# Time mixing on one core: low ranks from u and its shift difference, without their mixtures

## The chip, the cores and the metric

One core of a Trainium2 chip runs the whole program as one launch. The metric is device time in microseconds (us). The kernel before takes 2986.44 us, the median of 3 runs (2984.91 to 2988.6).

## What is computed

Two blocks follow each other on 512 tokens of width 1024, all in fp32. The change lies in the second block's first layer, in its time mixing; this is the part of it that matters:

```python
def rwkv7_time_mix(x, mu, w_rkv, w_o, w0, w1, w2, a0, a1, a2, g1, g2, ...):
    x_prev = jnp.pad(x, ((0, 0), (1, 0), (0, 0)))[:, :-1]
    xx = x_prev - x
    xr, xw, xk, xv, xa, xg = [x + xx * mu[i] for i in range(6)]
    r, k, v = xr @ w_rkv[0], xk @ w_rkv[1], xv @ w_rkv[2]
    w = -jax.nn.softplus(-(w0 + jnp.tanh(xw @ w1) @ w2)) - 0.5
    a = jax.nn.sigmoid(a0 + (xa @ a1) @ a2)
    g = jax.nn.sigmoid(xg @ g1) @ g2
    ...
```

`x` is the normalised input (`u` in the kernel) and `xx` its difference to the token before (`d`). w1 and a1 are 1024 x 64, g1 is 1024 x 128: these are the low ranks. After that a recurrence runs over the tokens for 16 heads of 64 (a matrix of state per head), its output is normalised per head, multiplied by `g`, and goes through the output projection `w_o`.

## The kernel before

**Layout and precision.** Activations lie as 8 chunks of 128 channels by 512 tokens. A large matmul is made of three passes in fp32r: a weight tile `wr` of 128 x 1024 comes by DMA, ACT rounds it to `wh`, DVE or POOL subtracts to get the rest `wl` (`wload`, line 406), and an activation is split into two halves in the same way. The low ranks go as plain fp32 matmuls, which the trace shows as two records each. All DMAs stand in one queue, SP's.

**An order that a planner writes.** The tasks are Python generators (`_Emit`, line 88 on). The main stream (the projections) emits its matmuls, and before each it lets other tasks that are due by the planner's own estimates emit theirs. So the order of the instructions on every engine, and in SP's queue, is fixed when the program is built; an instruction that is not ready holds up everything behind it on its engine. PSUM tiles of the main stream are called `m`, those of the tasks `t`. Tiles of 128 x 512 fp32, called `a`, come from a pool of 56 (`NA`, line 26); tasks that need many wait for room in it.

**Time mixing** (`rwkv`, from line 1096) goes over two halves of 256 tokens. `norm_task` (1137) makes for each half and chunk a tile with `u` in its first 256 columns and `d` in the others (`ud`). `ORDER` (1108) is the order of the projections: K, W, A, R, V, G of half 0, then of half 1. `mix_task` (1160) makes the mixtures u + mu*d, at most 8 tiles ahead of their use, on DVE by `mix_chunk` (1121): into `h` with a split for K, R and V, into half of an `a` tile without one for W, A and G. `token_major` (1185) projects K and V, `receptance` (1666) R, `lora1` (1203) the low ranks W, A and G from the mixtures, 8 matmuls each and half, 64 wide for W and A and 128 for G:

```python
for k in range(DC):
    x_ = take(hf, i, k)[0]
    w_ = w[k * m // 512][:, k * m % 512 : k * m % 512 + m]
    em.need(ps[:m, HW], w_, x_)
    mm(ps[:m, HW], w_, x_, k == 0, k == DC - 1)
```

The main loop (line 1724) walks through `ORDER`, loads low-rank weights one step ahead, and spawns `keys_task`, `decay_task`, `a_task`, `g_task` and `values_task`, which finish the projections and write them to DRAM.

**The recurrence** is a chain of tasks. `prep` (1358), for each of four blocks of 128 tokens `j` and each half of the heads `q`, fetches keys, `a`, decay and R (its first fetch is `a<-kkt`), makes products on DVE and PE, and writes `fsc`; it starts when the pool has room for 12 tiles (line 1524) and the one before the last is done. `inverse` (1451) reads `fsc` for both `q` as `iat`, runs 62 small operations on POOL, each after the one before, writes the result as `xsc`, reads it back, and finishes on PE with 32 x 32 matmuls. `scan_task` (1577) passes the state from chunk to chunk on tiles `sv`, `gn_task` (1531) normalises. Blocks 0 and 1 are half 0. `w_o` (1698) of half 0 needs both blocks of half 0 through `gn_task`; its matmuls carry `rwkv_w_o` in `wh`. `post` (1687) adds and normalises, and the feed-forward part of the layer follows, whose stages keep PE nearly full.

Below, stages are named by projection and half: K0, W0, A0, R0, V0, G0 and K1 to G1.

Of the kernel before, what the change touches and what calls it, by code (L numbers as in the profile page):

```python
# [20 lines left out]
P = 128  # L21
T = 512
D = 1024
DC = D // P
# [10 lines left out]
_VEC = {}  # L35
# [52 lines left out]
class _Emit:  # L88
# [209 lines left out]
def tile_net(ctx: ExitStack, tc: tile.TileContext, a: dict, out: bass.AP, dbg=None, stop=None):  # L298
# [101 lines left out]
    def copy(out_, in_, scale=None):  # L400
        if scale is None:
            act.activation(out=out_, in_=in_, func=AF.Copy)
        else:
            act.activation(out=out_, in_=in_, func=AF.Copy, scale=scale)
# [157 lines left out]
    t_ = H()  # L562
    gp.memset(t_, 0.0)
    copy(t_[:, 0:1], t_[:, 0:1])
    ps = PS()
# [531 lines left out]
    def rwkv(on_h):  # L1097
# [2 lines left out]
        live[0] = BEFORE  # L1100

        ud = {}
        oka, half_tile = S(), [None]
        vt.tensor_scalar(out=oka[:, 0:8], in0=vec[:, _VEC["k_a"] : _VEC["k_a"] + 8], scalar1=-1.0, scalar2=1.0, op0=MUL, op1=ADD)
        R_, W_, K_, V_, A_, G_ = range(6)
        LORA = {W_: ("w1", 64), A_: ("a1", 64), G_: ("g1", 128)}

        ORDER = [(0, K_), (0, W_), (0, A_), (0, R_), (0, V_), (0, G_), (1, K_), (1, W_), (1, A_), (1, R_), (1, V_), (1, G_)]
        LAST_A = [x for x in ORDER if x[0] == 0][-1]
        mixed = {x: [] for x in ORDER}  # L1110
        made, used, flags = [0], [0], {}
        AHEAD = 8
        EARLY = 10
        MARGIN = [2]
        turn = [0]

# [4 lines left out]
        def mix_chunk(i, c, hf):  # L1121

            uc, dc, m = ud[hf, c][:, 0:256], ud[hf, c][:, 256:512], V("mu", 8 * i + c)
            if i in LORA:
                if c % 2 == 0:
                    half_tile[0] = A()
                t_ = half_tile[0][:, HALF[c % 2]]
                vt.scalar_tensor_tensor(out=t_, in0=dc, scalar=m, in1=uc, op0=MUL, op1=ADD)
                return (t_,)
            t_ = H()  # L1130
            vt.scalar_tensor_tensor(out=t_, in0=dc, scalar=m, in1=uc, op0=MUL, op1=ADD)
            x_ = A(F32R)
            hi, lo = x_[:, 0:256], x_[:, 256:512]
            split_into((hi, lo), t_, HW, eng=vt if c % 3 == 2 else gp)
            return hi, lo
# [22 lines left out]
                free(*h, n=2)  # L1158

        def mix_task():  # L1160
            for hf, i in ORDER:
                for c in range(DC):
                    while made[0] >= used[0] + (AHEAD if (hf, i) in ORDER[:4] else 8) or (hf, c) not in ud or not room(MARGIN[0]):
                        yield 0.25
                    mixed[hf, i].append(mix_chunk(i, c, hf))
                    made[0] += i not in LORA or c % 2
                    if hf == 1 and i == ORDER[-1][1]:
                        free(ud[1, c])
                    if hf == 0 and (hf, i) == LAST_A:
                        free(ud[0, c])  # L1170
                    yield mixed[hf, i][max(c - 2, 0)]

        for hf in range(2):
# [7 lines left out]
        def take(hf, i, k):  # L1181
            em.until(lambda: len(mixed[hf, i]) > k)
            return mixed[hf, i][k]
# [16 lines left out]
            mixed[hf, i] = None  # L1200
            return pss

        def lora1(w, m, hf, i):
            ps = PS()
            for k in range(DC):
                x_ = take(hf, i, k)[0]
                w_ = w[k * m // 512][:, k * m % 512 : k * m % 512 + m]
                em.need(ps[:m, HW], w_, x_)
                mm(ps[:m, HW], w_, x_, k == 0, k == DC - 1)
                if k % 2:  # L1210
                    used[0] += 1
                    free(x_)
            mixed[hf, i] = None
            return ps

        def kkrow(wh):
# [58 lines left out]
            free(x_)  # L1275
            flags["lg", hf] = True

        def load_raw(src, n, rows=P):

            ts = [A() for _ in range(0, n, 512)]  # L1280
            for i, t_ in enumerate(ts):
                dma(out=t_[:rows, :], in_=src[:, 512 * i : 512 * i + 512])
            return ts

        def lora2(hf, w, rows, mid, done_):
            ws = load_raw(a[w], 1024, rows)
            for n in range(DC):
                p2 = PS()
                w_ = ws[n // 4][0:rows, (n % 4) * 128 : (n % 4 + 1) * 128]
                yield (p2, w_, mid)  # L1290
                mm(p2[:, HW], w_, mid[0:rows, :])
                done_(n, p2)
            free(*ws)

        def a_task(hf, ps):

            x_ = A()
            mid = x_[:, HW]
            copy(mid[0:64, :], ps[0:64, HW])

            def fin(n, p2):
                t_ = H()
                act.activation(out=t_, in_=p2[:, HW], func=AF.Sigmoid, bias=V("a0", n))
                spill(ad[hf][n], t_)

            yield from lora2(hf, "a2", 64, mid, fin)
            free(x_)
            flags["a", hf] = True

        def g_task(hf, ps):  # L1310

            x_ = A()
            mid = x_[:, HW]
            act.activation(out=mid, in_=ps[:, HW], func=AF.Sigmoid)

            def fin(n, p2):
                t_ = H()
                copy(t_, p2[:, HW])
                spill(gd[hf][n], t_)

            yield from lora2(hf, "g2", 128, mid, fin)
            free(x_)
            flags["g", hf] = True

# [394 lines left out]
            free(*(zq[hf, k][i] for k in range(4) for i in range(2)))  # L1719
            em.spawn(post(hf, o, hs, so))  # L1720

        tasks = {W_: decay_task, A_: a_task, G_: g_task}
        raw = {}
        for n, (hf, i) in enumerate(ORDER):
            for nxt in ORDER[n : n + 2]:
                if nxt[1] in LORA and nxt not in raw:
                    w, m = LORA[nxt[1]]
                    raw[nxt] = load_raw(a[w], 8 * m)
            if not hv and n >= EARLY and min(done["z"]) >= 1:
                w_o(0)  # L1730
            if i in LORA:
                em.spawn(tasks[i](hf, lora1(raw[hf, i], LORA[i][1], hf, i)))
                free(*raw[hf, i])
            elif i == K_:
                em.spawn(keys_task(hf, token_major(a["w_k"], K_, hf)))
            elif i == V_:
                em.spawn(values_task(hf, token_major(a["w_v"], V_, hf)))
            else:
                receptance(hf)
                if hf == 0:  # L1740
                    for q in range(2):
                        em.spawn(scan_task(q))
# [313 lines left out]
def _wn(w, ncol=512):  # L2056

    k, n = w.shape
    return np.ascontiguousarray(w.reshape(k // 128, 128, n // ncol, ncol).transpose(2, 1, 0, 3).reshape(n // ncol, 128, -1))
# [6 lines left out]
def pack(inp):  # L2066
    g = {k: np.asarray(v) for k, v in inp.items()}
    w = {}
# [44 lines left out]
    w["w_k"] = _wn(rkv[1])  # L2113
    w["w_v"] = _wn(rkv[2])
    w["rwkv_w_o"] = _wt(g["rwkv_w_o_2"][0])
    w["w1"] = _wn(g["rwkv_w1_2"][0], 64)[0]
    w["w2"] = np.ascontiguousarray(np.concatenate([g["rwkv_w2_2"][0], g["rwkv_w0_2"][0][None]], axis=0))
    w["a1"] = _wn(g["rwkv_a1_2"][0], 64)[0]
    w["a2"] = np.ascontiguousarray(g["rwkv_a2_2"][0])
    w["g1"] = _wn(g["rwkv_g1_2"][0], 128)[0]  # L2120
    w["g2"] = np.ascontiguousarray(g["rwkv_g2_2"][0])
# [28 lines left out]
```

## Time and profile before

| | |
|---|---|
| median of 3 runs | 2986.44 us |
| the profiled execution's own time | 2986.91 us |
| its span | 2985.1 us |
| PE busy | 2820.6 us (94%) |
| DVE, ACT, POOL busy | 1624.0, 1233.9, 692.3 us |
| mean granted TensorE clock | 0.968 of 2.4 GHz |

The profile is of one execution. Busy time is the time in which an engine had an instruction running; matmuls are pipelined and their ends are modelled, so a busy PE is not PE at its peak. The granted clock is 1 where TensorE ran at 2.4 GHz and 0.5 where it ran at 1.2 GHz; a value between is a mixture over the stretch. A wait is put down to the engine whose work was the last to be ready.

### The profile page before, as it was taken

What the parts mean: (1) busy time and instruction counts of PE and PEld (TensorE: products, weight loads), DVE (VectorE), ACT (ScalarE), POOL (GpSimd) and SP (SyncE); (2) the same over time, 40 slices, a digit from 0 to 9 for tenths busy, and PEclk for the clock granted to TensorE, in tenths of its full rate; (3) what the DMA queues carried; (4) which work ended last, traced back from release to release, by engine and by line L of the source; (5) the groups of instructions that cost most, each with busy time, mean ns of one, the idle gap of its engine ahead of it and who ended that gap; (6) DMA issues with size and microseconds to landing.
All of it is one profiled execution on the core that took longest, in us unless ns stands there. A gap on an engine that the chain in (4) does not pass through costs nothing. (4 is left out here: it accounts for less than half of the span.)

```text
span 2985.1 us, 45687 instructions
## 1 busy us (share of the span) xinstructions
PE 2820.6 (94%) x17736; PEld 2442.6 (82%) x17736; DVE 1624.0 (54%) x2896; ACT 1233.9 (41%) x2141; POOL 692.3 (23%) x802
## 2 busy tenths in 40 slices
PE   9999999999999989878789989998999989999998
PEld 7788888889888877656679989998888877888887
DVE  6545443335334486955676665366234476852336
ACT  4532333333333345544455544344233347733333
POOL 0022211111111143444355110111111134420111
PEclk9999999999999999988889999999999999999999
DMA  5333333332333455645565556343334432323334
GB/s 187 88 94 97 114 99 99 98 95 81 108 99 121 121 184 185 205 142 159 166 177 167 179 168 180 111 145 111 98 98 122 124 114 75 102 80 101 111 109 155
DMA packets 179408, 378.31 MB, mean 127 GB/s; under 512 B 57204, under 2 KB 81908, under 8 KB 179192
## 3 DMA queue, kind: packets, MB, share of 16 engines
q1 hardware_dynamic: 179192, 375.40, 41.6%
q8 instruction: 140, 2.29, 0.3%
q14 instruction: 76, 0.62, 0.1%
HBM read 342.04 MB, written 29.36 MB: 124 GB/s over the span
## 5 line engine op out<-in xcount | busy, mean ns | idle before, releaser
L379 PE MATMUL m<-a,wh 128*128 128x256 f32 (+1 forms) x8512 | 2061.5, 334 | 15.1 <-DVE a L290 7.2
L379 PEld LDWEIGHTS m<-a,wh 128*128 128x128 f32 x8512 | 1461.6, 192 | 178.7 <-issue 13.9
L379 PE MATMUL m<-a,wl 128*128 128x256 f32 (+1 forms) x4256 | 1414.1, 333 | 2.9 <-DVE wl L290 2.9
L290 ACT ACTIVATE wh<-wr 128x1024 fp32r<-128x1024 f32 (+2 forms) x585 | 606.0, 1038 | 1190.7 <-PE m L379 714.8
L290 DVE TENSOR_TENSOR wl<-wr,wh 128x1024 fp32r<-128x1024 f32 (+2 forms) x547 | 679.7, 1244 | 458.9 <-ACT wh L290 456.0
L379 PEld LDWEIGHTS m<-a,wl 128*128 128x128 f32 x4256 | 815.8, 192 | 78.4 <-DVE wl L290 3.5
L290 POOL TENSOR_TENSOR a<-a,a 128x256 f32<-128x256 f32 (+5 forms) x312 | 359.6, 1159 | 1633.5 <-ACT a L290 1317.4
L290 DVE TENSOR_TENSOR a<-m,a 128x512 f32<-128x512 f32 (+1 forms) x324 | 198.5, 614 | 629.6 <-PE m L379 618.9
L290 ACT ACTIVATE a<-a 128x512 f32<-128x512 f32 (+6 forms) x515 | 239.6, 481 | 121.3 <-DVE a L290 88.9
L379 PE MATMUL m<-wh,a 128*128 128x512 f32 x800 | 268.0, 409 | 12.5 <-DVE a L290 10.3
L379 PEld LDWEIGHTS m<-wh,a 128*128 128x128 f32 x800 | 155.7, 195 | 49.3 <-DVE a L290 12.5
L290 DVE TENSOR_TENSOR a<-a,a 128x256 f32<-128x256 f32 (+3 forms) x305 | 164.2, 567 | 36.0 <-ACT a L290 28.9
L379 PE MATMUL m<-wl,a 128*128 128x512 f32 x400 | 162.5, 406 | 0.0
L290 DVE SCALAR_TENSOR_TENSOR a<-a,vec,a 128x256 fp32r<-128x256 f32 (+4 forms) x246 | 144.9, 629 | 9.2 <-ACT a L290 8.4
L290 POOL TENSOR_TENSOR a<-h,a 128x256 fp32r<-128x256 f32 x80 | 68.3, 856 | 342.6 <-ACT a L290 328.0
L290 POOL TENSOR_TENSOR wl<-wr,wh 128x1024 fp32r<-128x1024 f32 x38 | 95.0, 2502 | 110.3 <-ACT wh L290 103.2
L379 PE MATMUL t<-a,a 64*128 64x128 f32 (+4 forms) x528 | 90.0, 356 | 32.0 <-DVE a L290 16.5
L379 PEld LDWEIGHTS t<-a,a 64*128 64x128 f32 (+3 forms) x528 | 57.4, 198 | 56.5 <-issue 25.6
L290 ACT ACTIVATE a<-t 128x512 f32<-128x512 f32 (+3 forms) x122 | 59.3, 491 | 90.0 <-PE t L379 70.6
L379 PEld LDWEIGHTS m<-wl,a 128*128 128x128 f32 x400 | 78.1, 195 | 16.1 <-issue 0.7
L290 ACT ACTIVATE a<-a,vec 128x256 fp32r<-128x256 f32 (+2 forms) x108 | 60.3, 565 | 47.2 <-DVE a L290 43.1
L292 ACT ACTIVATE a<-t 128x256 f32<-128x256 f32 (+3 forms) x100 | 45.4, 472 | 80.3 <-PE t L379 60.6
(108 smaller groups left out, 1533.5 us busy)
## 6 DMA issues: line engine op xcount, KB each, us to landing
wr<-in_ffn_w_in_dram SPq DMA_DIRECT2D x204, 512.0 KB, 3.7
wr<-in_ffn_w_out_dram SPq DMA_DIRECT2D x80, 448.0 KB, 3.3
wr<-in_ffn_w_out_dram SPq DMA_DIRECT2D x48, 512.0 KB, 3.6
wr<-in_w_out_t_dram SPq DMA_DIRECT2D x34, 512.0 KB, 3.7
wr<-in_w_mlp_in_dram SPq DMA_DIRECT2D x32, 512.0 KB, 3.6
wr<-in_w_mlp_out_dram SPq DMA_DIRECT2D x32, 512.0 KB, 3.7
wr<-in_w_gate_dram SPq DMA_DIRECT2D x16, 512.0 KB, 3.6
wr<-in_w_k_dram SPq DMA_DIRECT2D x16, 512.0 KB, 4.6
```

Source lines behind the costliest of these rows:

```text
L290: return fn(*args, **kw)
L292: return fn(*args, **kw)
L379: nc.tensor.matmul(out_, lhsT=lhsT, rhs=rhs, start=start, stop=stop)
```

## The change

W and A become one projection, and no low rank uses mixtures any more. Since (u + mu*d) @ w = u @ w + d @ (mu*w), the new `lora_w` fetches the weights `w` (w1 and a1 side by side in one packed array `wa1`, 128 columns for each chunk) and makes a second copy, scaled row by row by `mu`, on POOL; `lora1` then does 8 matmuls from `u` and 8 from `d` into one PSUM tile, 128 wide. W and A together keep 16 matmuls in each half; G has 16 instead of 8. The 48 mixtures of W, A and G on DVE fall away, and 12 multiplications on POOL come in: per half four of 128 x 4 x 64 for W and A, two of 128 x 512 for G. The weights of W and A are fetched and scaled at the start of K, those of G at the start of V. The `ud` tiles are now held until G of their half. `a_task` works on partitions 64 to 127. `ORDER` has 5 entries per half, and the mixing task goes through K, R and V only.

```diff
-        ORDER = [(0, K_), (0, W_), (0, A_), (0, R_), (0, V_), (0, G_), (1, K_), (1, W_), (1, A_), (1, R_), (1, V_), (1, G_)]
+        ORDER = [(hf, i) for hf in range(2) for i in (K_, WA_, R_, V_, G_)]
+        MIXED = [x for x in ORDER if x[1] in (K_, R_, V_)]
...
-            if i in LORA:
-                if c % 2 == 0:
-                    half_tile[0] = A()
-                t_ = half_tile[0][:, HALF[c % 2]]
-                vt.scalar_tensor_tensor(out=t_, in0=dc, scalar=m, in1=uc, op0=MUL, op1=ADD)
-                return (t_,)
...
-                    if hf == 1 and i == ORDER[-1][1]:
-                        free(ud[1, c])
-                    if hf == 0 and (hf, i) == LAST_A:
-                        free(ud[0, c])
...
+        def lora_w(name, idx):
+            ws = load_raw(a[name], 1024)
+            ms = []
+            for i, w_ in enumerate(ws):
+                m_ = A()
+                w4, m4 = (t_.rearrange("p (k i m) -> p k i m", k=4, i=len(idx)) for t_ in (w_, m_))
+                for x, id_ in enumerate(idx):
+                    c = _VEC["mu"] + 8 * id_ + 4 * i
+                    mu = vec[:, c : c + 4].unsqueeze(2).broadcast_to([P, 4, 128 // len(idx)])
+                    tt(gp, m4[:, :, x, :], w4[:, :, x, :], mu, MUL)
+                ms.append(m_)
+            return ws, ms
...
+        def lora1(hf, ws, ms):
             ps = PS()
             for k in range(DC):
+                em.until(lambda: (hf, k) in ud)
+                for i, t_ in enumerate((ws, ms)):
+                    w_, x_ = t_[k // 4][:, (k % 4) * 128 : (k % 4 + 1) * 128], ud[hf, k][:, HALF[i]]
+                    em.need(ps[:, HW], w_, x_)
+                    mm(ps[:, HW], w_, x_, k == 0 and i == 0, k == DC - 1 and i == 1)
+            free(*ws, *ms)
             return ps
...
         for n, (hf, i) in enumerate(ORDER):
+            if i == K_:
+                lw[WA_] = lora_w("wa1", (W_, A_))
+            elif i == V_:
+                lw[G_] = lora_w("g1", (G_,))
...
+            if i == WA_:
+                ps = lora1(hf, *lw[WA_])
+                em.spawn(decay_task(hf, ps))
+                em.spawn(a_task(hf, ps))
+            elif i == G_:
+                em.spawn(g_task(hf, lora1(hf, *lw[G_])))
+                free(*(ud[hf, c] for c in range(DC)))
```

With other tasks due at other times, the planner writes another order from K0 on. Three places of it follow.

On PE between K1 and R1: `m_10541` is W1 and `m_10434` the joined W1 and A1; the `t<-a,a 128x128` are a `prep`'s products. Before:

```order
L379 MATMUL m_10033<-wh_10453,a_10264 128x512
L379 MATMUL t_10480<-a_10425,a_10417 128x128 x4
L393 MATMUL t_10495<-cst,a_10417 128x128 x4
L379 MATMUL t_10595<-a_10503,a_10502 128x128 x4
L379 MATMUL t_10596<-a_10515,a_10502 128x128 x3
L379 MATMUL m_10541<-a_10279,a_10028 64x256 x2
```

Now:

```order
L379 MATMUL m_10083<-wh_10341,a_9975 128x512
L379 MATMUL t_10468<-a_10375,a_10374 128x128 x4
L379 MATMUL t_10469<-a_10387,a_10374 128x128 x4
L393 MATMUL t_10484<-cst,a_10374 128x128 x4
L393 MATMUL t_10590<-cst,a_10441 128x128 x4
L379 MATMUL m_10434<-a_8953,a_10070 128x256
L379 MATMUL m_10434<-a_8953,a_10074 128x256
```

The last `prep` ahead of the low ranks was the second one of block 1 and is now the first one of it; the second one of block 1 has moved to the end of R1.

In SP's queue at the store of the first inverse (`xsc_8655<-a`): `wr<-in_w_r` are R1's eight weight tiles. Before:

```order
L290 DMA a_10333<-rd_5551 128x4x128
L290 DMA xsc_8655<-a_9976 32x16x32 x4
L290 DMA wr_10761<-in_w_r_dram 128x1024
L290 DMA sv_10850<-vd_5557 64x4x64
L290 DMA sv_9599<-vd_5557 64x4x64
```

Now:

```order
L290 DMA sv_10950<-vd_5557 64x4x64 x2
L290 DMA sv_9587<-vd_5557 64x4x64 x2
L290 DMA wr_11038<-in_w_r_dram 128x1024
L290 DMA fsc_8652<-a_10264 32x8x32 x4
L290 DMA xsc_8655<-a_9911 32x16x32 x2
L290 DMA a_10506<-vt_5536 128x512
L290 DMA xsc_8655<-a_9911 32x16x32 x2
L290 DMA wr_11179<-in_w_r_dram 128x1024
```

All eight of R1's weights stood behind that store; now `wr_11038` is the fourth of four that stand ahead of it, and four stand behind.

On PE at the end of G1 (`m_12556`, now `m_11947`): `m_12707` is the first tile of `w_o` of half 0, and `t<-cst,a 32x32` the first PE step of an inverse, here that of block 1. Before:

```order
L379 MATMUL m_12556<-a_12208,a_11794 128x256 x2
L393 MATMUL t_12569<-cst,a_12557 128x128 x4
L393 MATMUL t_12604<-cst,a_12560 128x128 x4
L393 MATMUL t_12439<-cst,a_12416 128x128 x4
L393 MATMUL t_12639<-cst,a_12563 128x128 x4
L379 MATMUL t_12590<-a_12584,a_12586 128x256
L393 MATMUL t_12536<-cst,a_12513 128x128 x4
L379 MATMUL t_12714<-a_12626,a_12625 128x128 x4
L379 MATMUL t_12715<-a_12640,a_12625 128x128 x4
L393 MATMUL t_12730<-cst,a_12625 128x128 x4
L379 MATMUL m_12707<-a_11678,wh_12709 128x256
```

Now:

```order
L379 MATMUL m_11947<-a_9139,a_11630 128x256
L379 MATMUL m_11947<-a_9139,a_11635 128x256
L379 MATMUL t_12034<-cst,a_12030 32x32 x16
L379 MATMUL t_12050<-a_12044,a_12046 128x256
L379 MATMUL t_12095<-a_12044,a_12046 128x256
L379 MATMUL t_12100<-a_12044,a_12046 128x256
L379 MATMUL t_12090<-h_12087,a_10264 32x32 x16
```

Block 1's inverse and scan were finished on PE among the matmuls of R1 and V1, so that `w_o` came soon after G1; now they begin on PE only behind G1, and `w_o` behind them, with no main matmul in between (113 rows of `t` stand there).

## Rows read from the trace of the kernel before

**Rows 1.** The page: span, and granted clock in 40 equal slices, tenths.

```profile
span 2985.1 us, 45687 instructions
PEclk9999999999999999988889999999999999999999
```

**Rows 2.** Busy us (instructions) by stretch: length, PE, PEld, DVE, ACT, POOL, clock, DMA.

```profile
1087.00:1131.00 44.00, 31.23 (x117) 23.95 (x115) 40.19 (x89) 17.74 (x33) 22.29 (x23) 0.84 0.53 175
1131.00:1188.00 57.00, 51.73 (x313) 41.29 (x313) 34.40 (x59) 33.97 (x65) 19.80 (x19) 0.94 0.60 198
1188.00:1243.00 55.00, 42.25 (x213) 33.12 (x213) 52.68 (x91) 29.29 (x60) 25.34 (x23) 0.88 0.62 197
1276.00:1320.00 44.00, 25.68 (x149) 16.11 (x151) 27.56 (x58) 17.37 (x31) 15.12 (x31) 0.74 0.49 131
1320.00:1388.00 68.00, 64.11 (x748) 54.54 (x745) 34.00 (x61) 35.60 (x76) 43.44 (x74) 0.89 0.57 178
1388.00:1466.00 78.00, 62.98 (x676) 47.95 (x674) 53.25 (x115) 34.34 (x77) 19.57 (x18) 0.80 0.49 135
1466.00:1491.00 25.00, 12.87 (x57) 10.81 (x58) 14.59 (x45) 15.42 (x35) 12.34 (x29) 0.67 0.77 242
1529.00:1546.00 17.00, 9.09 (x152) 6.50 (x152) 14.07 (x35) 9.61 (x20) 1.76 (x2) 0.60 0.71 196
```

**Rows 3.** PE's waits, 1087 to 1546: us in total, times, longest us.

```profile
PE t L379 <- DVE a L290: 23.2, 13, 4.8
...
PE m L379 <- DVE a L290: 14.1, 6, 7.0
...
PE t L379 <- POOL a L290: 5.5, 1, 5.5
```

**Rows 4.** PE in order of time: start, length, records, [idle before <- releaser].

```profile
1131.45 7.12 PE L379 MATMUL m<-a,a 128*64 128x256 f32 x32 [2.18 <-DVE a L290]
...
1293.61 2.66 PE L379 MATMUL t<-a,a 64*128 64x128 f32 x14 [13.71 <-ACT a L290]
1296.20 6.11 PE L379 MATMUL m<-a,a 128*64 128x256 f32 x18
...
1391.40 0.69 PE L379 MATMUL t<-cst,a 32*32 32x32 f32 x32 [2.94 <-ACT a L292]
...
1474.71 5.23 PE L379 MATMUL m<-a,a 128*128 128x256 f32 x16 [9.61 <-ACT a L290]
...
1491.07 1.20 PE L379 MATMUL m<-a,wh 128*128 128x256 f32 x4
```

**Rows 5.** SP's queue in order of time around the first inverse's store.

```profile
1266.45 0.38 SPq L290 DMA_DIRECT2D a<-rd  x1
1285.24 1.95 SPq L290 DMA_DIRECT2D xsc<-a  x4
1287.23 0.51 SPq L290 DMA_DIRECT2D wr<-in_w_r_dram  x1
...
1303.24 0.82 SPq L290 DMA_DIRECT2D fsc<-a  x2
```

**Rows 6.** DVE groups by shape, 1060 to 1480: count, busy us, mean ns.

```profile
L290 DVE TENSOR_TENSOR wl<-wr,wh 128x1024 fp32r<-128x1024 f32 x32 | 39.9, 1246 | 21.4 <-ACT wh L290 21.0
...
L290 DVE SCALAR_TENSOR_TENSOR a<-a,vec 128x256 f32<-128x256 f32 x48 | 27.1, 595 | 0.1
```

**Rows 7.** POOL groups by shape, 1087 to 1491.

```profile
L290 POOL TENSOR_TENSOR wl<-wr,wh 128x1024 fp32r<-128x1024 f32 x22 | 56.8, 2580 | 63.1 <-ACT wh L290 57.6 <-DMA wr<-in_w_v_dram 4.5 <-DVE a L290 1.0
...
L292 POOL TENSOR_TENSOR a<-a,s 128x512 f32<-128x512 f32 x8 | 9.8, 1228 | 19.9 <-DVE s L292 13.9 <-ACT a L292 6.0
L290 POOL TENSOR_TENSOR a<-a,a 128x256 f32<-128x256 f32 x9 | 7.6, 848 | 3.7 <-ACT a L290 3.4
```

**Rows 8.** POOL in order of time: first and last of the 62 operations, two inverses.

```profile
1239.67 0.24 POOL L290 TENSOR_TENSOR h<-a,iat 128x31 f32<-128x31 f32 x1 [0.81 <-DMA iat<-fsc]
...
1284.98 0.23 POOL L290 TENSOR_TENSOR a<-a,h 128x16 f32<-128x16 f32 x1
...
1313.93 0.24 POOL L290 TENSOR_TENSOR h<-a,iat 128x31 f32<-128x31 f32 x1 [4.38 <-DMA iat<-fsc]
...
1381.09 0.29 POOL L290 TENSOR_TENSOR a<-a,h 128x16 f32<-128x16 f32 x1
```

More of the change, by code (lines that the diff above doesn't have):

```diff
@@ L1102, in rwkv @@
         ud = {}
-        oka, half_tile = S(), [None]
+        oka = S()
         vt.tensor_scalar(out=oka[:, 0:8], in0=vec[:, _VEC["k_a"] : _VEC["k_a"] + 8], scalar1=-1.0, scalar2=1.0, op0=MUL, op1=ADD)
         R_, W_, K_, V_, A_, G_ = range(6)
-        LORA = {W_: ("w1", 64), A_: ("a1", 64), G_: ("g1", 128)}
-        ORDER = [(0, K_), (0, W_), (0, A_), (0, R_), (0, V_), (0, G_), (1, K_), (1, W_), (1, A_), (1, R_), (1, V_), (1, G_)]
-        LAST_A = [x for x in ORDER if x[0] == 0][-1]
-        mixed = {x: [] for x in ORDER}
+        WA_ = 6
+        ORDER = [(hf, i) for hf in range(2) for i in (K_, WA_, R_, V_, G_)]
+        MIXED = [x for x in ORDER if x[1] in (K_, R_, V_)]
+        mixed = {x: [] for x in MIXED}
         made, used, flags = [0], [0], {}
         AHEAD = 8
-        EARLY = 10
+        EARLY = 8
         MARGIN = [2]
@@ L1160, in mix_task @@
         def mix_task():
-            for hf, i in ORDER:
+            for hf, i in MIXED:
                 for c in range(DC):
-                    while made[0] >= used[0] + (AHEAD if (hf, i) in ORDER[:4] else 8) or (hf, c) not in ud or not room(MARGIN[0]):
+                    while made[0] >= used[0] + (AHEAD if (hf, i) in MIXED[:2] else 8) or (hf, c) not in ud or not room(MARGIN[0]):
                         yield 0.25
                     mixed[hf, i].append(mix_chunk(i, c, hf))
-                    made[0] += i not in LORA or c % 2
-                    if hf == 1 and i == ORDER[-1][1]:
-                        free(ud[1, c])
-                    if hf == 0 and (hf, i) == LAST_A:
-                        free(ud[0, c])
+                    made[0] += 1
                     yield mixed[hf, i][max(c - 2, 0)]
@@ L1201, in token_major @@
             return pss
-        def lora1(w, m, hf, i):
+        def lora_w(name, idx):
[11 more added lines that the diff above has]
+        def lora1(hf, ws, ms):
             ps = PS()
             for k in range(DC):
[L1206 to L1213, printed above, removed]
+                em.until(lambda: (hf, k) in ud)
[4 more added lines that the diff above has]
+            free(*ws, *ms)
             return ps
@@ L1276, in decay_task, with load_raw @@
             flags["lg", hf] = True
-        def load_raw(src, n, rows=P):
+        def load_raw(src, n, rows=slice(0, P)):
             ts = [A() for _ in range(0, n, 512)]
             for i, t_ in enumerate(ts):
-                dma(out=t_[:rows, :], in_=src[:, 512 * i : 512 * i + 512])
+                dma(out=t_[rows, :], in_=src[:, 512 * i : 512 * i + 512])
             return ts
@@ L1288, in lora2 @@
                 p2 = PS()
-                w_ = ws[n // 4][0:rows, (n % 4) * 128 : (n % 4 + 1) * 128]
+                w_ = ws[n // 4][rows, (n % 4) * 128 : (n % 4 + 1) * 128]
                 yield (p2, w_, mid)
-                mm(p2[:, HW], w_, mid[0:rows, :])
+                mm(p2[:, HW], w_, mid[rows, :])
                 done_(n, p2)
@@ L1298, in a_task @@
             mid = x_[:, HW]
-            copy(mid[0:64, :], ps[0:64, HW])
+            copy(mid[64:128, :], ps[64:128, HW])
             def fin(n, p2):
@@ L1304, in fin @@
                 spill(ad[hf][n], t_)
-            yield from lora2(hf, "a2", 64, mid, fin)
+            yield from lora2(hf, "a2", slice(64, 128), mid, fin)
             free(x_)
@@ L1319, in fin @@
                 spill(gd[hf][n], t_)
-            yield from lora2(hf, "g2", 128, mid, fin)
+            yield from lora2(hf, "g2", slice(0, 128), mid, fin)
             free(x_)
@@ L1720, in w_o @@
             em.spawn(post(hf, o, hs, so))
-        tasks = {W_: decay_task, A_: a_task, G_: g_task}
-        raw = {}
+        lw = {}
         for n, (hf, i) in enumerate(ORDER):
[L1725 to L1728, printed above, removed]
+            if i == K_:
+                lw[WA_] = lora_w("wa1", (W_, A_))
+            elif i == V_:
+                lw[G_] = lora_w("g1", (G_,))
             if not hv and n >= EARLY and min(done["z"]) >= 1:
                 w_o(0)
-            if i in LORA:
-                em.spawn(tasks[i](hf, lora1(raw[hf, i], LORA[i][1], hf, i)))
-                free(*raw[hf, i])
+            if i == WA_:
[5 more added lines that the diff above has]
+                free(*(ud[hf, c] for c in range(DC)))
             elif i == K_:
@@ L2115, in pack @@
     w["rwkv_w_o"] = _wt(g["rwkv_w_o_2"][0])
-    w["w1"] = _wn(g["rwkv_w1_2"][0], 64)[0]
+    w["wa1"] = _wn(np.concatenate([g["rwkv_w1_2"][0], g["rwkv_a1_2"][0]], axis=1), 128)[0]
     w["w2"] = np.ascontiguousarray(np.concatenate([g["rwkv_w2_2"][0], g["rwkv_w0_2"][0][None]], axis=0))
-    w["a1"] = _wn(g["rwkv_a1_2"][0], 64)[0]
     w["a2"] = np.ascontiguousarray(g["rwkv_a2_2"][0])
```

## Prediction

> **What bounds the kernel now.** The page comes first: over the 2985.1 us span the granted clock falls below 0.9 only in the stretch of time mixing [rows 1]; elsewhere PE is full and nothing of this change is worked. The busy time by stretch is next [rows 2]. From 1087 to 1491 us, K0 to the start of `w_o`, PE is never full for long: it stands still for 12.8 us of 44 in K0, 12.8 of 55 in V0 and G0, 18.3 of 44 between K1 and R1, 15.0 of 78 in V1 and 12.1 of 25 around G1 (length less PE busy), and the clock there is 0.67 to 0.94. From 1087 to 1131 and from 1188 to 1243 DVE is busy 91% and 96% of the time: there DVE is the wall, and it is where the mixtures are made. The waits say the same [rows 3]: PE's largest totals are for DVE, 23.2 us by tasks and 14.1 us by the main stream. The fourth view is the order of time on PE, SP and POOL, which shows what stands between the projections [rows 4, 5, 8]; there a second limit shows. Block 1's inverse leaves POOL at 1381.4 (1381.09 + 0.29), its PE part starts at 1391.4, and `w_o` at 1491.1. So there are two chains into `w_o`: the main stream K0 to G1, and the blocks of the recurrence. They end nearly together, G1 at 1479.9 (1474.71 + 5.23).
>
> I work against the profiled execution: 2986.9 us, 1.8 us more than its span and 0.5 us above the median, so that a saving on it is a saving on the median.
>
> **K0 and W0.** DVE loses 48 mixtures of 595 ns, 27.1 us [rows 6], 16 of them by the end of W0. What counts is PE's waits. W0 waited 2.18 us for a mixture [rows 4]; `ud` is ready before. A one-column matmul of the norm waited 5.5 us for POOL [rows 3] with a third of K0 behind it; in the new order it stands behind 94 of K0's 96 matmuls. Together -7.7 us. W and A keep 16 matmuls; 64 or 128 columns of output make no difference that I count: 32 records take 7.12 us at 64 wide, and the 16 of G1, 128 wide, 5.23 us in a stretch of clock 0.67 [rows 2, 4], which is no less per record.
>
> **V0 and G0.** PE's longest wait on a DVE operand of the main stream, 7.0 us [rows 3], lies in V0, where DVE is 96% busy with `prep`; G's mixtures leave it, and V's are further ahead. I take it as gone, -7.0; below that, 0, if `prep` alone fills DVE. G's 8 added matmuls cost 16 records of 0.22 us (7.12/32): +3.5. Sum -3.5.
>
> **K1 to R1.** The largest single item. The 13.7 us [rows 4] are put down to ACT, but ACT was idle too: SP issued nothing from 1266.8 until the first inverse's store at 1285.2, and R1's first weights were queued behind that store [rows 5]; ACT's rounding of them stood ahead of the copy that PE wanted. In the new order four of R1's weights stand ahead of the store and the second `prep` of block 1 is no longer ahead of the low ranks. That wait goes: -13.7. W1 and A1 ran at the low clock, 6.11 us for 18 records where W0 took 7.12 for 32: with PE busy up to them, 32 records cost 7.1 instead of 10.9, by these two rows: -3.8. The moved `prep` matmuls and the transposes of K run in R1 as before, no gain and no loss. Sum -17.5. R1 ends 7.7 + 3.5 + 17.5 = 28.7 us earlier, at 1359.3 instead of 1388.
>
> **What is late next.** The chain of block 1. Its second `prep` now ends at the end of R1, because `prep` waits for room and the `ud` tiles and four weight tiles of a step stay live. From there: `fsc` to the first operation of the inverse, 10.7 us (1303.24 to 1313.93) [rows 5, 8]; the inverse itself, 45.5 us as the first one ran (1239.67 to 1285.21), or 67.5 as the second did, among more work [rows 8]; I take 47, near the first, since half as many splits stand between. Its end to PE, 10.0 us (1381.4 to 1391.4). Then PE part, two chunks of scan and the normalisation: before, 99.7 us (1391.4 to 1491.1), while PE did 63.0 us of work in V1 and 12.9 around G1 [rows 2]; without the main stream between, at least 99.7 - 75.9 = 23.8. I take 50, nearer the lower end, since V1 and G1 now lie ahead; DVE still has other blocks' `prep`. Together 118 us after R1 instead of 103 (1388 to 1491): +15. V1 and G1, with G's other 3.5 us, fit into the first 68 us of it and cost nothing; were that cover gone, they would cost up to 75.9. So `w_o` starts 28.7 - 15 = 13.7 us earlier.
>
> **POOL's new work.** Four multiplications of 256 columns at 0.85 us and two of 512 at 1.23 us per half [rows 7]: 5.9 us, 11.8 in both. Only G1's 2.5 us stand in block 1's inverse; they are in the 47. The 3.4 of W and A stand in the first inverse, whose store now holds back half of R1's weights only. Against this the Trainium skill (GPSIMD Engine Reference, section 4.1 Engine selection) puts elementwise work on a tile on VectorE, GPSIMD being about 2x slower for two inputs. The trace agrees in size: `wl` takes 2580 ns on POOL and 1246 on DVE [rows 6, 7]. By that rule the multiplications belong on DVE, the inverse would be some 2.5 us shorter and the sum 2.5 us lower; I leave that out.
>
> **Behind `w_o`.** From 1529 to 1546 PE waits for `post`: 9.1 us of work in 17 at clock 0.60 [rows 2]. In the new order the scan of block 2 stands in that gap, so that 7.9 us of standing still are filled by work that before lay in the feed-forward stretch, where PE is full: -7.9. A denser R0 to R1 also runs at a higher clock: R1 alone loses 0.11 of 68 us, 7.5 us; I take half, -4.
>
> **Sum.** -13.7 - 7.9 - 4 = -25.6: 2986.9 - 25.6 = 2961 us. Bounds: R1's end 15 to 40 us earlier (without V0's wait and the clock; or with half of the still-standing time up to there); the chain after R1 between 95 and 130 us; `post` 0 to -8. From these 2986.9 - 40 - 8 - 8 = 2931 and 2986.9 - 15 + 27 = 2999; the two ends that go together rarely I cut to 2992 above.
>
> **Rivals.**
> - The chain of block 1 takes over: its inverse runs among other work as the second one did (67.5 us, 20 more) and scan and normalisation need 70 instead of 50, since DVE has three `prep`s then and PE's clock is low after a still-stand, as around G1 (0.67). Then 158 us follow R1, `w_o` starts 26 us later than before, and with the 11.9 us behind it the time is 3001. It decides from 103 + 28.7 + 11.9 = 144 us on. For it: the second `prep` has moved a whole stage back. Against: POOL and DVE have less beside it. Chance 0.14.
> - DVE's time was hidden: where mixtures go, PE waits for `prep` on the same DVE, and 16 added matmuls cost 16 x 0.43 = 6.9 us. Of the terms only the 13.7 us of the queue stay; the chain's +15 and G0's 3.5 take them: 2986.9 - 13.7 + 15 + 3.5 = 2991.7. For it: DVE is 96% busy in V0 with mixtures only a small part. Chance 0.10.
> - More comes: the chain after R1 stays at 103 us because POOL and DVE are freer, so `w_o` gains all 28.7: 2986.9 - 28.7 - 11.9 = 2946. Chance 0.22.
> - The forecast, 2961, has 0.54.
>
> **Numbers.** A measurement of this kernel tells about 0.2%, 6 us, from no change. Faster by more: the forecast and the third rival, 0.76. Within 6 us: 0.10. Slower: 0.14. The range reaches from 2931 to 2992 and leaves out most of the slower case and a little below.
>
> **What would show it.** Right: no `a<-a,vec` mixtures on DVE; PE's 13.7 us wait gone and R1 beginning within 15 us of K1's end; R1 ending near 1359; a gap on PE behind G1 of some 30 to 45 us, released by POOL's inverse through the read of `xsc`; `w_o` starting near 1477; the scan of block 2 between `w_o` and the feed-forward part. Wrong: R1 ending later than 1375 (DVE was no wall), SP again standing still ahead of R1's weights, or more than 144 us between R1's end and `w_o`.

## The result, and the profile after

The changed kernel takes 3017.4 us, the median of 4 runs (3013.5 to 3023.5), beside 2987.1 of the kernel before in the same runs: a ratio of 1.0104, 95% interval 1.0082 to 1.0126. It is 30 us slower where 25 us faster was forecast. The profiled execution has a span of 3011.7 us, 26.6 us longer than before.

The page, the same two lines as [rows 1]: the granted clock now falls deeper, to between 0.7 and 0.8, in three slices of time mixing.

```profile
span 3011.7 us, 45698 instructions
PEclk9999999999999998897779999999999999999999
```

Busy time by stretch, columns as in [rows 2]: K0 to W0, V0 and G0, R1, from R1's end to block 1's inverse on PE, and from there to `w_o`.

```profile
1087.00:1141.00 54.00, 28.49 (x104) 21.49 (x105) 47.16 (x79) 20.52 (x40) 37.57 (x36) 0.76 0.51 171
...
1190.00:1243.00 53.00, 40.80 (x188) 32.21 (x187) 48.11 (x79) 25.25 (x55) 24.67 (x22) 0.81 0.43 129
...
1302.00:1368.00 66.00, 63.57 (x780) 53.29 (x779) 33.64 (x69) 38.70 (x79) 15.13 (x9) 0.97 0.77 235
1368.00:1453.00 85.00, 58.00 (x260) 45.26 (x261) 44.02 (x89) 30.90 (x64) 45.85 (x78) 0.76 0.44 127
1453.00:1538.00 85.00, 50.68 (x637) 41.60 (x632) 49.69 (x122) 33.74 (x86) 30.89 (x72) 0.70 0.45 128
```

PE in order of time, as in [rows 4]: ahead of W0; W1 with A1, and R1's start; R1's end; G1; the first step of block 1's inverse; the normalisation; `w_o`.

```profile
1123.68 1.02 PE L379 MATMUL t<-cst,a 128*128 128x1 f32 x4 [6.72 <-POOL a L290]
...
1131.82 1.22 PE L379 MATMUL t<-h,cst 128*128 128x256 f32 x2 [6.06 <-DVE h L292]
1136.43 1.12 PE L393 MATMUL t<-cst,a 128*128 128x128 f32 x4 [3.39 <-ACT a L290]
1140.57 1.65 PE L379 MATMUL m<-a,a 128*128 128x256 f32 x3 [3.03 <-DVE a L290]
...
1293.99 8.20 PE L379 MATMUL m<-a,a 128*128 128x256 f32 x32
1301.84 0.58 PE L379 MATMUL m<-a,wh 128*128 128x256 f32 x2
...
1367.72 0.35 PE L379 MATMUL m<-a,wl 128*128 128x256 f32 x1
...
1442.71 7.16 PE L379 MATMUL m<-a,a 128*128 128x256 f32 x24
...
1450.56 1.89 PE L379 MATMUL m<-a,a 128*128 128x256 f32 x8
...
1452.84 0.69 PE L379 MATMUL t<-cst,a 32*32 32x32 f32 x32 [0.39 <-DMA a<-xsc]
...
1521.05 1.12 PE L393 MATMUL t<-cst,a 128*128 128x128 f32 x4 [14.52 <-POOL a L292]
...
1533.66 2.07 PE L379 MATMUL t<-a,a 64*128 64x128 f32 x8 [9.48 <-ACT a L290]
...
1537.90 1.43 PE L379 MATMUL m<-a,wh 128*128 128x256 f32 x5 [1.13 <-ACT a L292]
```

The 13.71 us wait of [rows 4] is gone and R1 begins at 1301.8, 18.7 us earlier. In SP's queue the last of four weight tiles of R1 is now issued well ahead of the first inverse's store:

```profile
1280.43 0.56 SPq L290 DMA_DIRECT2D wr<-in_w_r_dram  x1
...
1298.40 0.95 SPq L290 DMA_DIRECT2D xsc<-a  x2
```

But `w_o` begins at 1537.9, 46.8 us later. What lies between is block 1. POOL in order of time: an operation of block 0's normalisation and block 1's inverse, first and last operation; then block 2's, with the normalisation's operations of block 1 (`a<-a,s`, L292) in the middle of it and behind it:

```profile
1386.93 1.04 POOL L292 TENSOR_TENSOR a<-a,s 128x512 f32<-128x512 f32 x1 [4.41 <-DVE s L292]
...
1388.91 0.38 POOL L290 TENSOR_TENSOR h<-a,iat 128x31 f32<-128x31 f32 x1
...
1432.73 0.23 POOL L290 TENSOR_TENSOR a<-a,h 128x16 f32<-128x16 f32 x1
...
1496.65 0.42 POOL L290 TENSOR_TENSOR h<-a,iat 128x31 f32<-128x31 f32 x1
...
1509.16 1.04 POOL L292 TENSOR_TENSOR a<-a,s 128x512 f32<-128x512 f32 x1
...
1519.78 1.22 POOL L292 TENSOR_TENSOR a<-a,s 128x512 f32<-128x512 f32 x1
...
1530.27 1.04 POOL L292 TENSOR_TENSOR a<-a,s 128x512 f32<-128x512 f32 x1
```

Before, this inverse ran from 1313.93 to 1381.4 [rows 8], beside R1; now it starts 75 us later, when R1 is over. SP's queue shows both ends of it. Ahead of it, the second `prep` of block 1 stores `fsc` 5.5 us behind R1's end. Behind it, the read-back of `xsc` stands behind the stores of V1 (`vd`, `vt`):

```profile
1373.59 0.93 SPq L290 DMA_DIRECT2D fsc<-a  x2
...
1376.85 1.11 SPq L290 DMA_DIRECT2D iat<-fsc  x2
...
1432.99 1.95 SPq L290 DMA_DIRECT2D xsc<-a  x4
1435.04 0.93 SPq L290 DMA_DIRECT2D wr<-in_rwkv_w_o_dram  x2
...
1446.24 0.86 SPq L290 DMA_DIRECT2D vt<-a  x2
1447.15 1.90 SPq L290 DMA_DIRECT2D a<-xsc  x2
```

V1's own matmuls were over at 1431.6. What its stores waited for is ACT, which copies V1's result: ahead of the last copies it had to round a weight tile of `w_o`, and that tile was fetched only behind the inverse's own store, at 1435.04:

```profile
1439.35 1.06 ACT L290 ACTIVATE wh<-wr 128x1024 fp32r<-128x1024 f32 x1 [8.52 <-DMA wr<-in_rwkv_w_o_dram]
```

PE stood still for those copies too (8.51 us, until 1440.95), and G1 came behind. G1's last matmuls ran until 1452.5, and they stand ahead of the inverse's first step on PE, which began at 1452.84. So an earlier read-back alone would have won 0.4 us: the two limits end together.

The change's own new work on POOL, by shape from 1087 to 1491, comes to 10.1 us, where I had 11.8:

```profile
L290 POOL TENSOR_TENSOR a<-a,vec 128x256 f32<-128x256 f32 x8 | 5.8, 751 | 2.8 <-DMA a<-in_wa_dram 2.8
...
L290 POOL TENSOR_TENSOR a<-a,vec 128x512 f32<-128x512 f32 x4 | 4.3, 1087 | 0.9 <-DMA a<-in_g_dram 0.9
```

### The profile page after: what moved, and what is told of

It is laid out like the page before. It is cut to its first block, busy times and chain, and to the rows that moved or that the text cites. A ratio compares the mean times of both kernels' runs of the same rounds, so it can differ in the third digit from the quotient of the medians.

```text
span 3011.7 us, 45698 instructions
## 1 busy us (share of the span) xinstructions
PE 2831.9 (94%) x17768; PEld 2460.3 (82%) x17768; DVE 1607.4 (53%) x2848; ACT 1234.3 (41%) x2141; POOL 698.0 (23%) x814
## 5 line engine op out<-in xcount | busy, mean ns | idle before, releaser
L379 PEld LDWEIGHTS t<-a,a 64*128 64x128 f32 (+3 forms) x528 | 65.0, 208 | 52.4 <-issue 22.8
L393 PE MATMUL t<-cst,a 128*128 128x128 f32 x256 | 47.3, 329 | 35.1 <-POOL a L292 17.5
```

The source lines that it names most:

```text
L393: nc.tensor.transpose(out_, in_, ident[: in_.shape[0], : in_.shape[0]])
```

## The experiments

Theory A: the loss is the place of block 1's second `prep`; the tiles that the change holds longer take its room, and all of block 1 follows later. Theory B: the added work. Theory C: any other order that the planner writes is worth tens of us either way. All ran against the kernel before, on the same chip as those of their group. The table has three readings of each profiled execution (first operation of block 1's inverse on POOL, first matmul of `w_o`, span), then the median of all runs and its ratio to the kernel before. us:

| run | inverse 1 | w_o | span | median | ratio, 95% interval |
|---|---|---|---|---|---|
| before | 1313.9 | 1491.1 | 2985.1 | 2987.1 | |
| change | 1388.9 | 1537.9 | 3011.7 | 3017.4 | 1.0104 (1.0082 to 1.0126) |
| e1 change, room 8 | 1307.4 | 1465.9 | 2966.5 | 2975.5 | 0.9960 (0.9945 to 0.9975) |
| e2 W and A only | 1404.4 | 1548.7 | 3038.4 | 3032.2 | 1.0160 (1.0144 to 1.0176) |
| e3 before, ud held | 1332.4 | 1490.5 | 2990.7 | 2991.1 | 1.0011 (1.0001 to 1.0021) |
| e4 before, room 8 | 1306.8 | 1490.9 | 2985.6 | 2982.1 | 0.9985 (0.9976 to 0.9994) |
| e5 weights late | 1316.6 | 1508.5 | 3009.5 | 3011.3 | 1.0074 (1.0057 to 1.0091) |
| e6 normalisation on DVE | 1385.5 | 1522.1 | 3003.3 | 3008.3 | 1.0067 (1.0052 to 1.0082) |
| e7 scaling on DVE | 1393.2 | 1549.7 | 3040.5 | 3042.4 | 1.0181 (1.0166 to 1.0197) |
| e8 room 8, e6, late norm | 1307.2 | 1463.4 | 2957.3 | 2957.8 | 0.9911 (0.9883 to 0.9939) |
| e9 change, room 11 | 1313.3 | 1486.3 | 2990.3 | 2991.5 | 1.0004 (0.9993 to 1.0014) |
| e10 before, edits of e8 | 1307.6 | 1473.5 | 2967.5 | 2963.2 | 0.9908 (0.9890 to 0.9927) |
| e11 room 8, e6 | 1313.5 | 1484.7 | 2986.5 | 2988.5 | 1.0000 (0.9990 to 1.0010) |
| e12 e2, room 11 | 1388.1 | 1533.8 | 3024.8 | 3026.5 | 1.0125 (1.0108 to 1.0142) |
| e13 room 8 for block 1 | 1311.4 | 1470.1 | 2985.9 | 2987.7 | 0.9993 (0.9982 to 1.0003) |
| e14 before, late prep | 1427.1 | 1542.7 | 3027.0 | 3031.4 | 1.0147 (1.0133 to 1.0161) |
| e15 before, room 16 | 1380.4 | 1521.6 | 3001.2 | 3011.6 | 1.0089 (1.0064 to 1.0113) |
| e16 room 8, late norm | 1311.2 | 1491.3 | 2986.8 | 2976.3 | 0.9958 (0.9944 to 0.9972) |
| e17 e8 again | 1309.0 | 1468.0 | 2961.4 | 2962.5 | 0.9912 (0.9899 to 0.9926) |
| e18 e10 again | 1301.5 | 1467.7 | 2960.2 | 2965.2 | 0.9929 (0.9908 to 0.9951) |

Read the second column first: there are two groups with nothing between, 1301 to 1333 (with R1) and 1380 to 1427 (after it). All seven of the second are slower than before, by 0.7% (20 us) and more; of the first, all but e5 lie between 2958 and 2992. That is a scatter of 34 us within the first group, as wide as the loss itself, so theory A rests on the two groups together and on e14 and e15 below, not on the size of any single gain.

**e1, e9: the room for `prep`.**

```diff
-                while n >= prepped[0] + 2 or not room(12):
+                while n >= prepped[0] + 2 or not room(8):
```

> The changed kernel with one number changed: prep starts when the pool has room for 8 tiles instead of 12. Theory A (room: the ud tiles that are held until G and the four weight tiles of each low rank keep the second prep of block 1 out of the pool until R1 is over, and all of block 1's chain with it): that prep starts ahead of W1 and A1 again, the 170 us between R1's end and w_o come down to 100 to 130, and the time comes down by 25 to 50 us, to 2967 to 2992. Theory B (the added work itself: 16 matmuls of G, 12 multiplications on POOL): nothing of that is touched, so the time stays at 3010 to 3020. Theory C (any other order of the planner is worth some 10 us up or down, whatever the room): 3005 to 3030.

2975.5, as A said and below the kernel before. POOL's first operation of block 1's inverse, its first step on PE and `w_o` in e1:

```profile
1307.39 0.24 POOL L290 TENSOR_TENSOR h<-a,iat 128x31 f32<-128x31 f32 x1 [0.45 <-DMA iat<-fsc]
```

```profile
1386.16 1.06 PE L379 MATMUL t<-cst,a 32*32 32x32 f32 x32 [6.07 <-DMA a<-xsc]
...
1465.89 0.50 PE L379 MATMUL m<-a,wh 128*128 128x256 f32 x2 [1.43 <-ACT a L292]
```

No multiplication, matmul or transfer is taken away here, so B falls as the main cause.

> The changed kernel with room for 11 tiles instead of 12: the smallest step. Theory A (room): prep of block 1 takes the same early place as with room for 8, and the time is 2965 to 2988. Theory C (any other order is worth tens of us either way): it comes out anywhere, 2960 to 3040, and 3000 or more would speak against A.

With 11 it is 2991.5, 3.5 us above A's range: the chain is back in its place and 26 of the 30 us with it, but not the rest that e1 gained.

**e13: the same for block 1 alone** (`room(8 if j == 1 else 12)`).

> The changed kernel with room for 8 for the two preps of block 1 alone; all the others still wait for 12. Theory A (the place of block 1's preps is the loss): block 1's inverse begins on PE at 1380 to 1405 instead of 1453 and the time is 2965 to 2992. If the gain of the first run came from the later preps' earlier start: 3000 or more.

2987.7: the whole loss is taken back by moving the two `prep`s of block 1. The 12 us by which e1 is better lie in the other `prep`s, the only difference.

**e14, e15: the loss inflicted on the kernel before.**

```diff
-                while n >= prepped[0] + 2 or not room(12):
+                while n >= prepped[0] + 2 or not room(12) or (n == 3 and not flags.get(("r", 1, 1))):
```

> The kernel before with one condition more: the second prep of block 1 waits until R1 has been given out, where the change has put it. No arithmetic, no weights and no tiles differ. Theory A: block 1's inverse begins on PE at 1440 to 1480 and the time is 3010 to 3045. If the late chain does not matter: 2984 to 2995.

> The kernel before with room for 16 tiles instead of 12, that is four tiles scarcer for prep alone, about what the four weight tiles of a low rank take. Theory A: the second prep of block 1 starts a stage later, block 1's inverse begins on PE at 1410 to 1460, and the time is 2995 to 3025. Otherwise 2984 to 2993.

Both times are as A said: 3031.4 and 3011.6. In e14 PE reads `xsc` 89 us later than before (1480.54, just past the range, against 1391.40 [rows 4]):

```profile
1427.10 1.28 POOL L290 TENSOR_TENSOR h<-a,iat 128x31 f32<-128x31 f32 x1 [13.06 <-DMA iat<-fsc]
```

```profile
1298.71 0.50 PE L379 MATMUL m<-a,wh 128*128 128x256 f32 x2
...
1480.54 1.07 PE L379 MATMUL t<-cst,a 32*32 32x32 f32 x32 [5.40 <-DMA a<-xsc]
...
1542.69 0.58 PE L379 MATMUL m<-a,wh 128*128 128x256 f32 x1
```

This is the strongest pair: nothing of the change is in e14, and it is slower than the change. It delays more than the change does, though: its inverse starts 38 us later than the change's. e15 (`room(16)`) shows that a count of four tiles is enough; its inverse starts within 9 us of the change's, and it loses 0.9% (27 us). The row at 1298.71 shows one thing more: e14 makes every mixture and still begins R1 at 1298.7, earlier than the change. So R1's earlier start comes with the moved `prep` as well and is not shown to be the mixtures' doing.

**e3, e4: held tiles alone, and the control.** Both are the kernel before; e4 has room 8 and nothing else.

```diff
-                    if hf == 1 and i == ORDER[-1][1]:
-                        free(ud[1, c])
-                    if hf == 0 and (hf, i) == LAST_A:
-                        free(ud[0, c])
...
                 free(*raw[hf, i])
+                if i == G_:
+                    free(*(ud[hf, c] for c in range(DC)))
```

> The kernel before with one part of the change alone: the ud tiles are held until G of their half instead of going free as the last mixtures are made. Theory A: prep of block 1 finds room later, by some 5 to 15 us, and w_o with it: 2992 to 3002. Theory B: no work is added, 2984 to 2990.

> The kernel before with room for 8 instead of 12, the control for the first: if fewer tiles of room help by themselves, they help here too. Theory A: here prep of block 1 waited little for room, so little changes: 2977 to 2995. If the time falls by 20 us or more, the first run's gain is not the change's own loss taken back.

e3 costs 3 to 4 us (2991.1), a little under A's range: holding `ud` moves the inverse by 18 us, still beside R1. e4 gains 4 to 5, so e1's 42 us are the change's own loss for the most part.

**e5: the weights not held ahead.**

```diff
-            if i == K_:
-                lw[WA_] = lora_w("wa1", (W_, A_))
-            elif i == V_:
-                lw[G_] = lora_w("g1", (G_,))
...
             if i == WA_:
+                lw[WA_] = lora_w("wa1", (W_, A_))
...
             elif i == G_:
+                lw[G_] = lora_w("g1", (G_,))
```

> The changed kernel with the weights of a low rank fetched and scaled at its own step instead of one projection ahead, so that four tiles fewer stand in the pool during K and during V; room for 12 stays, and the ud tiles are still held until G. Theory A1 (it is the weights held ahead that kept prep of block 1 out): that prep starts ahead of W1 and A1, 85 to 120 us lie between R1's end and w_o, and the time is 2970 to 2995, a few us of it lost where W0 and G wait for their weights. Theory A2 (it is the held ud tiles): R1's end to w_o stays near 170 us and the time at 3008 or more.

Neither: the time is 3011.3, yet the inverse is back at 1316.6. So it was the four weight tiles (with `ud` held, as here, the `prep` found its place), and A1 is right on the mechanism and wrong on the price: W1 and A1 began at 1306.6 instead of 1294.0, R1 ended at 1398.8 instead of 1368.1 (1380.2 in e1, where block 1 lies beside it as here), and G1 waited for ACT and for its own scaled weights:

```profile
1488.14 1.22 PE L379 MATMUL m<-a,a 128*128 128x256 f32 x2 [9.05 <-ACT a L290]
1493.94 3.78 PE L379 MATMUL m<-a,a 128*128 128x256 f32 x8 [4.58 <-POOL a L290]
```

**e2, e12: W and A alone**, with G from mixtures as before (`lora1m` is `lora1` of the kernel before, and `mix_chunk` makes G's mixtures again); e12 adds `room(11)`.

```diff
-                lw[G_] = lora_w("g1", (G_,))
+                lw[G_] = load_raw(a["g1"], 1024)
...
-                em.spawn(g_task(hf, lora1(hf, *lw[G_])))
-                free(*(ud[hf, c] for c in range(DC)))
+                em.spawn(g_task(hf, lora1m(lw[G_], 128, hf, G_)))
+                free(*lw[G_])
```

> The changed kernel with G made from mixtures as in the kernel before (the ud tiles go free when G's mixtures are made, 8 matmuls of G per half, no scaling of its weights); W and A stay joined, from u and d. Theory A: four tiles of weights of W and A still stand in the pool during K1, and in this kernel too the second prep of block 1 finds room for 12 only during R1; 3005 to 3025, not much better than the change. Theory B: half of the added matmuls and a third of the multiplications go, and with them more than half of the loss: 2990 to 3002.

> The second run (W and A joined, G from mixtures, 3032) with room for 11 instead of 12. Theory A: prep of block 1 starts ahead of W1 and A1, 2972 to 2995, some 40 us less. If the added 8 mixtures per half and not the room made it 3032, it stays above 3010.

3032.2 is worse than either theory had it. e12 missed its aim: with room for 11 the inverse still starts at 1388.1, and 3026.5 agrees with that place. It tells nothing of the mixtures' cost.

**e6: the normalisation's two operations on DVE** (`tt(gp, y3, ...)` to `tt(vt, y3, ...)`).

> The changed kernel with the two 128x512 operations of the normalisation (subtract the mean, multiply by the factor) on DVE instead of POOL; room and weights as changed. If the 14.5 us for which PE waited on a POOL operation of the normalisation, and the 8.5 us behind it, come from the inverse of block 2 in POOL's queue, they go, w_o comes 10 to 20 us earlier and the time is 2996 to 3010. If the normalisation only waited for what was late anyway, 3011 to 3022.

3008.3, as expected if the two waits came from POOL's queue: some 9 us of the loss were the normalisation standing behind block 2's inverse on POOL. In its trace the waits at that place are 6.49, 3.20 and 3.17 us, all for DVE, in place of 14.52 and 9.48, and `w_o` starts 15.8 us earlier.

**e7: the scaling on DVE.**

> The changed kernel with the 12 scaling multiplications on DVE instead of POOL, nothing else. Theory A (room): they lie beside other work, so 3005 to 3020, and only PE's 6.7 us wait for POOL ahead of W0 shrinks. Theory B (POOL's added work is the loss): 2990 to 3003. By the rule of the Trainium skill that I weighed in the prediction it would be some 2.5 us lower than the change, 3015.

3042.4, 25 us slower than the change and outside all three. The multiplications themselves are cheaper there, 6.5 us instead of 10.1:

```profile
L290 DVE TENSOR_TENSOR a<-a,vec 128x256 f32<-128x256 f32 x8 | 3.7, 517 | 2.2 <-DMA a<-in_wa_dram 2.2
...
L290 DVE TENSOR_TENSOR a<-a,vec 128x512 f32<-128x512 f32 x4 | 2.8, 726 | 0.0
```

W0 begins no earlier for it (1141.5 against 1140.6). So 12 multiplications moved made the planner write an order in which `w_o` starts 12 us later still. That is theory C; that it makes all of the scatter within the two groups is argued, not shown.

**e8, e11, e16, e10, e17, e18: a better version, and what the change is worth in it.** e8 has room for 8, e6's edit, and the norm of the second half held until W0 and A0 are given out; e11 is without that last, e16 without e6's edit; e10 is the kernel before with all three; e17 and e18 are e8 and e10 side by side.

```diff
+    def late(gen):
+        def task():
+            while not went:
+                yield 0.25
+            yield from gen
...
                 ps = lora1(hf, *lw[WA_])
+                went.append(1)
```

> A candidate to beat both: the changed kernel with room for 8, the normalisation's two operations on DVE, and the norm of the second half held back until W0 and A0 have been given out (so that its two small matmuls stand behind them on PE and not ahead). Against the first experiment (2975): the 19 us that PE stood still ahead of W0 go in part, 5 to 15 us, if DVE and POOL have the norm's sums ready later without new waits; the normalisation on DVE is worth 0 to 5. 2957 to 2972. If K1 then waits for the late norm, 2975 to 2985.

> The best version without the late norm: the changed kernel with room for 8 and the normalisation on DVE. Between 2958 and 2975: by the 19 us that PE stood still ahead of W0 with the early norm and 12 with the late one, the late norm is worth some 4 to 8 us, so 2961 to 2967; the rest is the normalisation's.

> The changed kernel with room for 8 and the late norm, the normalisation on POOL as before. Against the first run (2975, no late norm) and the best one (2958, with the normalisation on DVE too): if the late norm makes the gain, 2955 to 2965; if it takes both, 2968 to 2985.

> The kernel before with the three edits of the best version so far (2958): room for 8, the normalisation's two operations on DVE, and the norm of the second half behind A0. What the change itself is worth once the order is mended: by the first and the fourth run (2975 against 2982) some 7 us, so 2960 to 2972 here. At 2958 or less the change is worth nothing by itself.

> The best version again (changed kernel, room for 8, normalisation on DVE, late norm): 2955 to 2970.

> The kernel before with the same three edits again, on the same chip as the run ahead of it: 2958 to 2970. If the change is worth something in itself it lies 4 to 12 us above that run; if not, within 3 us or below.

e8 is the fastest, 2957.8, and 2962.5 when repeated (e17): 0.9912 of the kernel before. But the three edits do not add. On top of room for 8, the late norm alone gives nothing (e16 2976.3, its profile being that of its slowest run; e1 2975.5), the normalisation alone loses 13 us (e11 2988.5), and both gain 13 to 18. I had taken each for a term of its own, and e11 missed its range (up to 2975) by 13 us for it; they act as orders again. What the change is worth in the mended order is read from two pairs. e10 took 2963.2, 5 us above e8 (on another chip) and inside the range that I had given for a change worth some 7 us. e18 took 2965.2 beside e17's 2962.5 on the same chip, inside the 3 us that I had given for a change worth nothing, and the intervals overlap. Both pairs lie on the change's side: **in a mended order the change is worth a few us at most, and these runs do not show that it is worth anything.**

## Why the prediction was wrong

**K0 and W0: wrong sign.** -7.7 was forecast; R0 ended 2.6 us later (1189.6 against 1187.0). The step that failed is "in the new order it stands behind 94 of K0's 96": I took a wait as gone because little of K0 was left behind it, but W0 was. Four waits of 6.72, 6.06, 3.39 and 3.03 us, 19.2 in all, stand ahead of W0, in place of the 7.7 (5.5 and 2.18) that were to go. W0 and A0 began 9.1 us later and took 9.84 us instead of 7.12, at a clock of 0.72. R0 gave 9.2 us of it back: it took 39.2 us without a wait at clock 1.00, where it had taken 48.4 at 0.93.

**V0 to R1: the sum right, the split wrong.** From R0's end to R1's start it was 133.5 us, and is 112.2: -21.3 against -3.5 - 17.5 = -21.0. That the two agree is luck. V0 gave none of its 7.0: from R0's end to G0's start it took 53.8 us instead of 48.6. PE's waits from 1188 to 1243, two groups before and one after (`m` the main stream, `t` the tasks):

```profile
PE m L379 <- DVE a L290: 7.0, 1, 7.0
PE t L379 <- DVE a L290: 3.7, 3, 2.1
...
PE t L379 <- DVE a L290: 10.7, 5, 4.2
```

The main stream's 7.0 us went as forecast, but PE waits for DVE as long as before, 10.7 us in all, now for `prep`: DVE stayed busy 48.1 of 53 us. That is what the second rival said. K1 to R1 gave more than forecast: from G0's start to R1's start it took 58.4 us instead of 84.9. Its mechanism, R1's weights ahead of the `xsc` store, held, but by e14 it is not shown to need the change. R1 ended at 1368.1, 8.8 us behind the forecast's 1359.3 and still 19 us earlier than before (1386.8).

**The chain after R1: the right mechanism at the wrong size, and this is the error that turned the sign.** The prediction had the second `prep` end at R1's end for want of room; it ended 5.5 us behind it, and e13 to e15 show that its place makes the loss. The step that failed is the length of what follows. It gave 118 us; it took 169.8 (1368.1 to 1537.9):

| term | forecast | measured |
|---|---|---|
| R1's end to the inverse's first operation | 10.7 | 20.8 |
| the inverse on POOL | 47 | 44.1 |
| its end to PE | 10.0 | 19.9 |
| PE part, scan, normalisation, to `w_o` | 50 | 85.1 |

The first: `fsc` was stored 5.5 us behind R1's end, and from there to the inverse it took 15.3 us instead of 10.7, because on POOL a split and an operation of block 0's normalisation, which waited 4.41 us for DVE, stood ahead of it; the data had landed by 1381.6.

The third: I carried over the 10 us of [rows 4, 8], though SP's queue in between had changed, and I let V1 and G1 "fit into the first 68 us" and "cost nothing", though by my own rows they held up to 75.9 us of PE's work. They ended 84.3 us after R1 (1452.5). V1 began only at 1392.4, behind matmuls of the tasks; then PE waited 5.97 us for a split that stood among block 1's inverse on POOL, and 8.51 us for ACT. The first three rows together are 84.8 us, so what failed here is the cover as much as the read-back.

The fourth is the largest, 35 us. I took 50 "nearer the lower end, since V1 and G1 now lie ahead", as if PE's other work were all that had stretched it. But PE was busy only 50.7 of the 85 us, at a clock of 0.70: it waited, 14.52 us for the normalisation behind block 2's inverse on POOL and 9.48 for ACT, which itself waited 12.39 us for the next operation of the normalisation, behind the same inverse:

```profile
1531.35 0.63 ACT L292 ACTIVATE a<-a 128x512 f32<-128x512 f32 x1 [12.39 <-POOL a L292]
```

e6 gives 9 us of it back; the rest of the 35 is not divided further.

**Behind `w_o`: right in sign.** From `w_o` to the end it is 1473.8 us instead of 1494.0: -20.2, against -7.9 for `post`. The other -4 was for a higher clock from R0 to R1. It did rise, in R0 (part of the 9.2 us that R0 gave back) and in R1's stretch from 0.89 to 0.97, but R1 took 66 us both times. What makes up the 20.2 was not followed. And 46.8 - 20.2 = 26.6, the difference of the two spans.

**POOL's new work** was sized rightly (10.1 for 11.8 us) and is not the cause: without it on POOL (e7) the time is no better. The Trainium skill (GPSIMD Engine Reference, section 4.1 Engine selection) would put it on VectorE. The trace agrees in direction, DVE taking 517 and 726 ns where POOL takes 751 and 1087; but e7 was 25 us slower where I had the rule give 2.5, so for the kernel's time the measurement decides against it.

**The rival that came true** is the first, the chain of block 1 taking over. It needed more than 144 us after R1; there were 170. But half of its mechanism did not come: it had the inverse at 67.5 us, which took 44.1, and scan and normalisation at 70, which took 85.1. Its price, 3001, was 16 us too low, and its chance of 0.14 looks too small: the moved `prep` stood in the order, and the sum gave 15 us for it where the kernel before, with the inverse late, loses 27 (e15) to 44 us (e14).

What stays open: in e13 `w_o` starts 21 us earlier than before, and the span is still the same; which waits behind `w_o` take the 21 us was not followed. Why e5's R1 ends so late is only begun above. And why room for 11 brings the `prep` forward in the change but not in e12 was not followed either.

## What to carry to other kernels

Where a program's order is planned from a count of free buffers, a buffer that is held longer is a cost on whatever task waits for room, and that task's whole chain has to be priced at its new place, each of its waits anew. A term carried over from the old order (10 us from the inverse's end to PE, 5.5 us of waiting that "goes") is the one to doubt. Before crediting an arithmetic saving, look for the one event that the end follows: here each us at the start of `w_o` was worth 0.8 us of span over the twenty rows of the table (a straight line through them, with e13 16 us off it), whatever the arithmetic was. And a single edit to a planned program is judged against controls: the same delay in the old program, the same mending in both.

## What the runs showed that I had not expected

- Giving each operation to its faster engine lost time twice: scaling on DVE (10.1 to 6.5 us of work) cost 25 us, and the normalisation on DVE, at room for 8, 13.
- The inverse of a block, the same 62 operations on POOL, takes 44.1 us behind R1 in the change, 38.9 in e14, and 67.5 beside R1 in the kernel before. Between its operations POOL did 10 us of other work in the change, none in e14, and 20 us in the kernel before, where it also stood still for 25. It is shortest where the kernel is slowest: an engine that is free of other work can be a sign that the chain stands alone.
